# Strassen's seven products in the output projection of a hybrid attention and recurrence layer

## The chip, the core and the metric

The kernel runs on one NeuronCore of a Trainium2 chip. Its engines work side by side, each through its own queue in order: TensorE (PE, with its weight loads shown apart as PEld), VectorE (DVE), ScalarE (ACT), GpSimd (POOL) and SyncE (SP), which issues most of the transfers. The metric is the device time of one execution in microseconds (us), lower is better.

## The reference

One encoder layer, x of 512 positions by 2048 channels in float32. Cut to what matters here:

```python
h = rms_norm(x, norm_w)
q, k, v, g_attn, xr, g_lru = split(h @ w_in)          # w_in: 2048 x 4608
attn = attention_group(q, k, v)                        # 8 heads of 128, 2 key/value heads
lru = lru_group(xr)                                    # conv, gates, scans in both directions
mixed = concat([rms_norm(attn, attn_norm_w) * silu(g_attn),
                rms_norm(lru, lru_norm_w) * silu(g_lru)])   # 512 x 2048
out = x + mixed @ w_out                                # w_out: 2048 x 2048
```

## The kernel before

**Numbers.** Every product is float32 in three passes (`mm3`, L111): each operand is split into a high part (ScalarE rounds it, L168) and a low part (VectorE subtracts, L169), and TensorE adds high by high, high by low and low by high in one PSUM bank. PSUM is cut into four banks named pj, for the projections, and four named mm, for all else.

**Order.** The order of TensorE's instructions is that of the program text (a manual schedule, L599). The other engines are put in order by a scheduler when the program is built. Weights come in chunks of 256 rows by 512 columns (`wload`, L172), three raw buffers deep, and a loop over chunks (`proj_feat`, L239; `tok_block`, L259) gives way after each six matmuls of 512 columns. Such a group of six is called a step of filling here: `weave` (L274) runs a chain of other work and fills it with those steps.

**Stages.** (1) The rows of x are turned and normalised, and the first half of the recurrence's input is projected. (2) The recurrence runs between the projections of its second half, of keys and values, and of the queries. After the second block of queries `norm_rope` (L438) normalises and rotates it: per tile of 128 positions ScalarE squares (L446), GpSimd takes the root (`rsqrt_mean`, L218), and VectorE runs L451, L453 twice, L459 and L460. (3) `group_rstd` (L585) sums the recurrence's squares over channels on TensorE (L589), VectorE copies the result (L593) and GpSimd takes the root: r_l, one number for each position. (4) `attention` (L544) goes over 32 pairs of head and block of queries: scores (L507), a maximum (L509), exponentials (L512), a reciprocal (L513), a product on GpSimd (L514), transposes two pairs later (L521), products with the values one pair after that, as matmuls of 256 columns (L531). Between two pairs stand `STEPS = 3` steps of filling from the four blocks of gate projections (`all_gates`, L667). (5) r_a is made in the same way from the attention's squares (L688), the 16 blocks of the mixed features are split (`mixed`, L580), and the output projection runs (L694 to L708): for each of four blocks of 512 columns and each of the two groups, 96 matmuls of 512 columns go into four banks, and VectorE then adds them to x with r_l or r_a as the factor of each position:

```python
for c in range(DM // SEQ):
    for half, r in ((1, r_l), (0, r_a)):
        drain(tok_block(acc, w_out, half * 8 * P, c * SEQ, mh[half * 8 :], ml[half * 8 :], 8))
        ...
        nc.vector.scalar_tensor_tensor(part[t], acc[t], r[:, t : t + 1], part[t], ...)
```

The norm of each group is thus applied behind the product, and TensorE waits for neither r_l nor r_a.

## Time and profile before

| | us |
|---|---|
| median of 3 runs | 683.5 (683.4 to 683.67) |
| the profiled execution, its own time | 681.98 |
| its span, first to last instruction | 680.2 |
| TensorE busy within the span | 668.9 |
| VectorE, ScalarE, GpSimd busy | 407.5, 317.8, 74.4 |
| output projection, first to last matmul | 501.57 to 675.75 |

Durations of single instructions come from the profiled execution. A matmul's duration in it includes its way through the array, so that neighbours overlap: the distance from start to start is what a stream of them costs. A VectorE instruction, too, begins a little before the one ahead of it has ended.

### The profile page before, as it was taken

The page shows a single profiled execution, that of the slowest core. Times are in us where ns is not written, and L with a number is a line of the kernel's source. Part 1 is how long each engine was busy: PE and PEld are TensorE (multiplying, and loading weights), DVE is VectorE, ACT ScalarE, POOL GpSimd, SP SyncE. Part 2 cuts the span into 40 slices and gives each one's busy share as a digit, 9 for nine tenths or more (in the row PEclk, how much of TensorE's full clock was granted, in tenths as well). Part 3 has the DMA queues.
Part 4 walks back from the last instruction along what each step waited for, and adds up shares of the span by engine and source line. Part 5 has one row for each costly group of instructions (what it writes and reads, how often), then busy time and mean ns, then how long its engine had stood idle before and what let it go on. Part 6 is the DMA issues. An engine that isn't in the chain of part 4 may idle for free.

```text
span 680.2 us, 8576 instructions
## 1 busy us (share of the span) xinstructions
PE 668.9 (98%) x3154; PEld 555.2 (82%) x3154; DVE 407.5 (60%) x713; ACT 317.8 (47%) x593; POOL 74.4 (11%) x84
## 2 busy tenths in 40 slices
PE   8999999999989999999999999999999999999997
PEld 6888888887778888888888888888888888888885
DVE  5878697978495824856744774576475334443342
ACT  4534898588945427444634643464452222222220
POOL 0000001200150203201211111112000000000000
PEclk9999999999999999999999999999999999999999
DMA  8852242213123332222112122122256362522411
GB/s 281 279 155 75 82 131 89 66 62 94 62 75 112 100 98 81 93 64 65 61 63 92 51 74 63 62 63 76 81 173 202 109 227 93 155 93 93 160 58 63
DMA packets 43626, 71.01 MB, mean 104 GB/s; under 512 B 2760, under 2 KB 12864, under 8 KB 43584
## 3 DMA queue, kind: packets, MB, share of 16 engines
q1 hardware_dynamic: 43552, 70.45, 32.1%
q8 instruction: 25, 0.41, 0.3%
q14 instruction: 17, 0.14, 0.1%
q10 hardware_dynamic: 32, 0.01, 0.0%
HBM read 66.25 MB, written 4.19 MB: 104 GB/s over the span
## 4 chain that ended last, share of the span: by engine, by line
PE 85%; DVE 7%; ACT 4%; issue 2%; DMA 1%; SPq 0%; ACTq 0%; DVEq 0%
PE pj L113 24%; PE pj L112 24%; PE pj L114 24%; PE mm L114 3%; PE mm L113 3%; PE mm L112 3%; PE mm L521 2%; DVE b L399 2%; DVE wl L169 2%; DVE k L355 1%; PE mm L194 1%; ACT wh L168 1%; ACT b L388 1%; DMA b<-in_x_dram 1%; DVE b L396 1%
## 5 line engine op out<-in xcount | busy, mean ns | idle before, releaser
L169 DVE TENSOR_TENSOR wl<-wr,wh 128x512 fp32r<-128x512 f32 x208 | 145.4, 712 | 163.2 <-ACT wh L168 163.0
L168 ACT CAST wh<-wr 128x512 fp32r<-128x512 f32 x208 | 126.5, 620 | 209.5 <-PE pj L114 154.6
L112 PE MATMUL pj<-wh,x 128*128 128x512 f32 x448 | 175.1, 391 | 2.8 <-ACT ev L434 2.8
L113 PE MATMUL pj<-wl,x 128*128 128x512 f32 x448 | 174.8, 390 | 1.9 <-DVE wl L169 1.8
L114 PE MATMUL pj<-wh,x 128*128 128x512 f32 x448 | 174.5, 390 | 0.0
L112 PE MATMUL pj<-x,wh 128*128 128x512 f32 x384 | 152.9, 398 | 0.0
L114 PE MATMUL pj<-x,wl 128*128 128x512 f32 x384 | 150.0, 391 | 0.0
L113 PE MATMUL pj<-x,wh 128*128 128x512 f32 x384 | 149.9, 390 | 0.0
L112 PEld LDWEIGHTS pj<-wh,x 128*128 128x128 f32 x448 | 84.1, 188 | 21.3 <-ACT ev L434 3.6
L113 PEld LDWEIGHTS pj<-wl,x 128*128 128x128 f32 x448 | 84.1, 188 | 20.0 <-DVE wl L169 2.9
L114 PEld LDWEIGHTS pj<-wh,x 128*128 128x128 f32 x448 | 84.1, 188 | 17.4
L114 PEld LDWEIGHTS pj<-x,wl 128*128 128x128 f32 x384 | 72.1, 188 | 15.5
L113 PEld LDWEIGHTS pj<-x,wh 128*128 128x128 f32 x384 | 72.3, 188 | 13.9 <-issue 0.2
L112 PEld LDWEIGHTS pj<-x,wh 128*128 128x128 f32 x384 | 72.2, 188 | 14.0 <-issue 0.2
L523 ACT CAST b<-mm 128x512 fp32r<-128x512 f32 x32 | 18.8, 587 | 71.8 <-PE mm L521 71.8
L514 POOL TENSOR_SCALAR k<-k,sm 128x512 f32<-128x512 f32 x32 | 26.1, 817 | 157.4 <-DVE sm L513 139.1
L509 DVE TENSOR_REDUCE mx<-mm 128x1 f32<-128x512 f32 x32 | 22.0, 688 | 30.7 <-PE mm L114 30.6
L524 DVE TENSOR_TENSOR b<-mm,b 128x512 fp32r<-128x512 f32 x32 | 22.0, 689 | 10.5 <-ACT b L523 10.5
L408 POOL TENSOR_TENSOR hsum<-hsum,b 128x512 f32<-128x512 f32 x7 | 13.4, 1909 | 122.3 <-ACT b L407 122.3
L512 ACT ACTIVATE k<-mm,mx 128x512 f32<-128x512 f32 x32 | 22.1, 692 | 4.3 <-DVE mx L509 3.9
L372 ACT ACTIVATE b<-mm,vec 128x512 f32<-128x512 f32 x32 | 21.2, 687 | 1.2 <-PE mm L114 0.9
L320 DVE TENSOR_TENSOR ev<-pj,rbc 128x512 f32<-128x512 f32 x24 | 16.4, 689 | 6.5 <-PE pj L114 6.3
(136 smaller groups left out, 698.3 us busy)
## 6 DMA issues: line engine op xcount, KB each, us to landing
wr<-in_w_in_dram SPq DMA_DIRECT2D x71, 512.0 KB, 3.4
wr<-in_w_out_dram SPq DMA_DIRECT2D x32, 512.0 KB, 3.6
k<-in_x_dram SPq DMA_DIRECT2D x16, 256.0 KB, 5.2
out_dram<-k SPq DMA_DIRECT2D x16, 256.0 KB, 3.6
b<-in_x_dram SPq DMA_DIRECT2D x7, 512.0 KB, 8.3
k<-in_lru_wa_dram SPq DMA_DIRECT2D x8, 128.0 KB, 3.4
k<-in_lru_wx_dram SPq DMA_DIRECT2D x8, 128.0 KB, 2.9
b<-in_x_dram SPq DMA_DIRECT2D x2, 256.0 KB, 5.1
```

What stands on the lines that cost most here:

```text
L112: nc.tensor.matmul(acc, lh, rh, start=start, stop=False)
L113: nc.tensor.matmul(acc, lh, rl, start=False, stop=False)
L114: nc.tensor.matmul(acc, ll, rh, start=False, stop=stop)
L168: nc.scalar.copy(hi, raw[:, k, :])
L169: nc.vector.tensor_sub(lo, raw[:, k, :], f(hi))
L320: nc.vector.tensor_mul(e, a, rbc)
L372: nc.scalar.activation(dst[:, d, :], pg, AF.Sigmoid, bias=v1(bias + d * NB + n))
L509: nc.vector.tensor_reduce(mx, sc, axis=AX.X, op=ALU.max, negate=True)
L512: nc.scalar.activation(p, sc, AF.Exp, bias=mx, accum_out=sm)
L514: nc.gpsimd.tensor_scalar(p, p, sm, 0.0, op0=ALU.mult, op1=ALU.add)
L523: nc.scalar.copy(pth[:, :, tt], p3)
L524: nc.vector.tensor_sub(ptl[:, :, tt], p3, f(pth[:, :, tt]))
```

## The change

**Output projection** (`outputs`). The 16 blocks of 128 mixed features are taken in eight pairs. For one block of 512 output columns, a pair's product is that of a matrix of 2 by 2 blocks (position half by feature block) with one of 2 by 2 blocks (feature block by column half). Six of the eight pairs use seven products in place of eight, the other two use eight. Each product is made of 128-row stationary tiles and moving tiles of 256 columns. All products go into eight PSUM banks, four pj and four mm; the seven-product pairs share seven of them, and are combined after the sixth pair (L740 to L747). The operands need sums and differences of blocks: for the features (`build`) once, for the weights (`seven`, with `combine`) again for each chunk, on VectorE.

**Norms.** Since both groups now add into the same banks, r_l and r_a are multiplied into the features ahead of the product. `rows` (new) spreads r over all partitions: VectorE writes r times the identity (L260, four times), TensorE multiplies it by a matrix of ones (L262), VectorE copies the result to gbc (L263), and `normed` multiplies the pairs by it.

**Attention** has `STEPS = 2`; the fourth block of gates runs after it. **SBUF** is cut into pools that are opened and closed along the program, where a new tile waits only for the old tiles that it covers.

```diff
-STEPS = 3
+STEPS = 2
+    def rows(dst, col, dg):
+        for t in range(NT):
+            nc.vector.tensor_scalar(dg[:, t, :], ident, col[:, t : t + 1], None, op0=ALU.mult)
+        pb = mm()
+        nc.tensor.matmul(pb, ones, dg.rearrange("p t q -> p (t q)"), start=True, stop=True)
+        nc.vector.tensor_copy(dst, pb)
...
+    def normed(pair):
+        nc.vector.tensor_mul(pair, pair, gbc[:, None, :].broadcast_to([P, 2, SEQ]))
+    P1, Q6, Q5, Q7, P2, Q3, Q4 = (0, 0), (5, 5), (4, 3), (3, 4), (2, 2), (6, 1), (1, 6)
+    def combine(src, op):
+        res = pools["fin"].tile([P, 4, H], F32, tag="t4", bufs=2, name=nm("t4"))
+        a = nc.vector.tensor_tensor
+        if op == ALU.add:
+            a(res[:, 0:2], src[:, 1:3], src[:, 0:1].broadcast_to([P, 2, H]), op=op)
+            a(res[:, 2], res[:, 0], src[:, 2], op=op)
+            a(res[:, 3], res[:, 2], src[:, 3], op=op)
...
+    def seven(src, op, hi, lo):
+        src = halves(src)
+        res = combine(src, op)
+        for to, part in ((slice(0, 3), src[:, 1:4]), (slice(3, 7), res)):
+            nc.scalar.copy(hi[:, to], part)
+            nc.vector.tensor_sub(lo[:, to], part, f(hi[:, to]))
+    def outputs(work):
+        for c in range(DM // SEQ):
+            xt = pools["out"].tile([P, 4, 2, H], F32, tag="xt", bufs=1, name=nm("xt"))
...
+            for q, (ts_, cs) in enumerate(spots):
+                nc.sync.dma_start(xt[:, q], xf[ts_, cs].rearrange("(s p) e -> p s e", p=P))
+            acc = {k: pj() for k in (P1, Q6, Q5, Q7)} | {k: mm() for k in (P2, Q3, Q4, 0)}
...
+            for i, (r0, A) in enumerate(mixed):
...
+                if i < 6:
+                    for k in (P1, Q6, Q5, Q7, P2, Q3, Q4):
+                        for s in range(2):
+                            mult(k, s, ah, al, k[0], bh, bl, k[1], i == 5 and k in (P1, Q6, Q5, Q7))
+                else:
+                    for k, a, b_ in (
+                        (P2, (1, 3), (1, 3)), (Q3, (1, 3), (0, 2)),
+                        (Q4, (0, 2), (1, 3)), (0, (0, 2), (0, 2)),
+                    ):
...
+                if i == 5:
+                        nc.scalar.copy(comb[:, 0], acc[P1])
+                        nc.vector.tensor_sub(v2, acc[Q6], comb[:, 0])
+                        nc.vector.tensor_add(comb[:, 1], acc[Q5], v2)
+                        nc.vector.tensor_add(comb[:, 2], acc[Q7], comb[:, 1])
...
+                        nc.vector.tensor_add(xt, xt, comb)
+                for k, q in ((P2, 0), (Q3, 1), (Q4, 3), (0, 2)):
+                    nc.vector.tensor_add(xt[:, q], acc[k], xt[:, q])
+                    nc.sync.dma_start(of[ts_, cs].rearrange("(s p) e -> p s e", p=P), xt[:, q])
...
-    r_l = group_rstd(hsum, "r_l", NB * P)
-    fill = all_gates()
+    r = group_rstd(sums["l"], "r_l", NB * P)
+    rows(gbc, r, pools["rot"].tile([P, NT, P], F32, tag="sq", bufs=2, name=nm("sq")))
+    closed("rot", "rope")
+    opened("att", "right")
+    for pair in hp:
+        normed(pair)
+    fill = gates()
     weave(fill, attention(rots))
-    drain(fill)
-    r_a = group_rstd(asum, "r_a", NH * HD)
+    for _ in range(6):
+        next(fill)
+    r = group_rstd(sums["a"], "r_a", NH * HD)
+    next(fill)
+    rows(gbc, r, fin_s((P, NT, P)))
```

In the built program three places look as follows. The first is TensorE at the end of the second block of queries (its last matmul is the first row), before:

```order
L114 MATMUL pj_2082<-wh_2343,x_87_478 128x512
L589 MATMUL mm_2447<-ones,hsum 128x1 x4
L471 MATMUL mm_2457<-ident,ev_2003 128x128
L471 MATMUL mm_2457<-ident,ev_2005 128x128
L471 MATMUL mm_2457<-ident,ev_2007 128x128
```

and now:

```order
L145 MATMUL pj_2099<-wh_2360,x_87_489 128x512
L621 MATMUL mm_2464<-ones,hsum 128x1 x4
L262 MATMUL mm_2478<-sq_2473,ones 128x512
L507 MATMUL mm_2492<-ident,ev_2020 128x128
L507 MATMUL mm_2492<-ident,ev_2022 128x128
```

The matmul L262, which reads the tile sq_2473 that VectorE writes, has come between the sums of squares and the transposes of the queries.

The second place is VectorE at the same time, where ev_... are the four tiles of the second block of queries in `norm_rope`. Before, from the third and fourth tile's work on:

```order
L169 TENSOR_TENSOR wl_2570<-wr_2563,wh_2569 128x512
L460 TENSOR_TENSOR ev_2373<-ev_2373,sq_2429 128x512
L453 TENSOR_TENSOR sq_2435<-ev_2375,rq 128x8x32 x2
L451 TENSOR_TENSOR ev_2377<-ev_2377,rr_2412 128x512
L459 TENSOR_TENSOR ev_2375<-ev_2375,rq 128x512
L453 TENSOR_TENSOR sq_2441<-ev_2377,rq 128x8x32
L460 TENSOR_TENSOR ev_2375<-ev_2375,sq_2435 128x512
...
L459 TENSOR_TENSOR ev_2377<-ev_2377,rq 128x512
L169 TENSOR_TENSOR wl_2611<-wr_2608,wh_2610 128x512
...
L460 TENSOR_TENSOR ev_2377<-ev_2377,sq_2441 128x512
```

and now:

```order
L489 TENSOR_TENSOR sq_2452<-ev_2392,rq 128x8x32 x2
L487 TENSOR_TENSOR ev_2394<-ev_2394,rr_2429 128x512
L495 TENSOR_TENSOR ev_2392<-ev_2392,rq 128x512
L489 TENSOR_TENSOR sq_2458<-ev_2394,rq 128x8x32
L496 TENSOR_TENSOR ev_2392<-ev_2392,sq_2452 128x512
...
L260 TENSOR_SCALAR sq_2473<-ident,r_l 128x128
L495 TENSOR_TENSOR ev_2394<-ev_2394,rq 128x512
...
L496 TENSOR_TENSOR ev_2394<-ev_2394,sq_2458 128x512
L260 TENSOR_SCALAR sq_2473<-ident,r_l 128x128 x2
L263 COPY gbc<-mm_2478 128x512
L632 TENSOR_TENSOR hs_861<-hs_861,gbc 128x1024
```

The four instructions L260 that L262 reads stand at the end of the queries' normalisation (they write to the buffer of an earlier sq tile); the splits of the next weights (L169, now L200) have moved behind them.

The third place is TensorE where the output projection begins, before (x_923 and x_924 are the high and low part of a block of features):

```order
L113 MATMUL pj_4166<-x_87_477,wh_4530 128x512
L114 MATMUL pj_4166<-x_86_477,wl_4531 128x512
L589 MATMUL mm_4582<-ones,asum 128x1 x4
L112 MATMUL pj_4655<-wh_4661,x_923_4591 128x512
L113 MATMUL pj_4655<-wl_4662,x_923_4591 128x512
L114 MATMUL pj_4655<-wh_4661,x_924_4592 128x512
```

and now (mh and ml are those parts):

```order
L144 MATMUL pj_4364<-x_87_489,wh_4637 128x512
L145 MATMUL pj_4364<-x_86_488,wl_4638 128x512
L704 MATMUL pj_4683<-wh_4693,mh_4237 128x256
L704 MATMUL pj_4683<-wl_4694,mh_4237 128x256
L704 MATMUL pj_4683<-wh_4693,ml_4238 128x256
```

The matmuls have half the columns, and there are 1392 of them (464 of each of the three kinds) where there were 768.

More of the change, by code (lines that the diff above doesn't have):

```diff
@@ L640, in hybrid_kernel @@
     s1.close()
+    sums["l"] = pools["rope"].tile([P, SEQ], F32, tag="hsum", name="hsum")
     lru_consts()
@@ new lines, in hybrid_kernel, with build @@
+    fill = gates()
+    weave(fill, attention(rots))
+    for _ in range(6):
+        next(fill)
+    r = group_rstd(sums["a"], "r_a", NH * HD)
+    closed("att", "qkv")
+    opened("fin", "right")
+    next(fill)
+    rows(gbc, r, fin_s((P, NT, P)))
+    mixed = [[(NH + 2 * q) * P, None] for q in range(4)] + [[2 * q * P, None] for q in range(4)]
+    def build(i, pair, where, n=7):
+        mixed[i][1] = hi, lo = where(n)
+        if n == 7:
+            seven(pair, ALU.subtract, hi, lo)
+        else:
+            four(pair, hi, lo)
@@ new lines, in hybrid_kernel, with later @@
+    for q in range(4):
+        for _ in range(2):
+            next(fill, None)
+        build(q, hp[q], lambda n: kept(pools["fin"]))
+    drain(fill)
+    def later():
+        for pair in ap_[:2]:
+            normed(pair)
+        yield 6
+        todo = gate(late, ap_[:2], R_AN, fin_s)
+        for _ in range(3):
+            yield next(todo)
+        build(4, ap_[0], lambda n: [hring.tile([P, n, H], F32R, name=nm(t)) for t in ("mh", "ml")])
+        yield from todo
+        for pair in ap_[2:]:
+            normed(pair)
@@ new lines, in hybrid_kernel, with last_gates @@
+    acc = []
+    fill = proj_feat(C_GA + SEQ, acc)
+    weave(fill, later())
+    drain(fill)
+    gs = evac_bc(acc)
+    closed("xw")
+    opened("out", "left")
+    def last_gates():
+        yield
+        build(5, ap_[1], lambda n: kept(pools["out"]))
+        yield
+        todo = gate(gs, ap_[2:], R_AN + 4, fin_s)
+        for _ in range(3):
+            next(todo)
+        yield
+        build(6, ap_[2], lambda n: kept(pools["out"], n), 4)
+        drain(todo)
+        yield
+        build(7, ap_[3], lambda n: kept(pools["out"], n), 4)
+        yield
```

241 lines of the change are left out of this document (155 added, 86 removed).

## The prediction

> **What bounds the kernel now.** I read the page first: the busy times and the chain that ended last.
>
> ```profile
> span 680.2 us, 8576 instructions
> PE 668.9 (98%) x3154; PEld 555.2 (82%) x3154; DVE 407.5 (60%) x713; ACT 317.8 (47%) x593; POOL 74.4 (11%) x84
> PE 85%; DVE 7%; ACT 4%; issue 2%; DMA 1%; SPq 0%; ACTq 0%; DVEq 0%
> ```
>
> TensorE is busy for 668.9 of 680.2 us and makes up 85% of the chain. So a change pays only by taking work from TensorE, and anything that makes TensorE wait costs its full length. The second view is the output projection by itself: the stretch from its first to its last matmul, with the instructions that touch pj alone (columns: length, then busy time and count of PE, PEld, DVE).
>
> ```profile
> 501.57:675.75 174.18, 174.18 (x768) 144.07 (x768) 23.83 (x32) 0.00 (x0) 1.00 0.39 129
> ```
>
> 768 matmuls of 512 columns fill 174.18 us without a gap, 0.2268 us each, at full clock. The third view is the timeline of TensorE where the old kernel already runs the new shape, 256 columns with a stationary tile loaded for each (attention's values).
>
> ```profile
> 309.04 0.36 PE L112 MATMUL mm<-b,v 128*128 128x256 f32 x1
> 309.24 0.28 PE L113 MATMUL mm<-b,v 128*128 128x256 f32 x1
> 309.35 0.28 PE L114 MATMUL mm<-b,v 128*128 128x256 f32 x1
> ...
> 310.37 0.28 PE L114 MATMUL mm<-b,v 128*128 128x256 f32 x1
> 310.48 0.40 PE L112 MATMUL pj<-x,wh 128*128 128x512 f32 x1
> ```
>
> From the second matmul's start to that of the next group are 11 steps in 1.24 us: 0.113 us each. With its entry the group of 12 takes 1.44 us, 0.120 each.
>
> **1. The output projection.** Six pairs of seven products are 42 matmuls each, two pairs of eight are 48 each: 348 for a column block, 1392 in all. At half of 0.2268 us they take 157.9 us; the saving is 174.2 - 157.9 = **16.3 us**. Bounds: 17.3 us at 0.1127, 7.1 us at 0.120. I take the half, since a long stream is nearer to the inside of that group than to its entry.
>
> **2. Cover of that stream.** One column block is 39.5 us of TensorE, a seven-product pair 4.77 us. VectorE's work beside it comes from these groups.
>
> ```profile
> L169 DVE TENSOR_TENSOR wl<-wr,wh 128x512 fp32r<-128x512 f32 x208 | 145.4, 712 | 163.2 <-ACT wh L168 163.0
> L168 ACT CAST wh<-wr 128x512 fp32r<-128x512 f32 x208 | 126.5, 620 | 209.5 <-PE pj L114 154.6
> L396 DVE TENSOR_TENSOR b<-b,b 128x1024 f32<-128x1024 f32 x8 | 9.6, 1215 | 0.0
> L459 DVE TENSOR_TENSOR ev<-ev,rk 128x256 f32<-128x256 f32 x4 | 1.7, 416 | 0.0
> L704 DVE SCALAR_TENSOR_TENSOR k<-pj,r_a,k 128x512 f32<-128x512 f32 x16 | 12.0, 750 | 11.0 <-PE pj L114 10.9
> ```
>
> A chunk of weights for seven products takes 0.71 + 2 x 0.42 (sums) + about 0.96 (768 columns) + 1.22 = 3.7 us; six make 22.4, the other two 2.4. Combining takes 4 x 0.75, the sum of 2048 columns 2.4, the last four sums 3.0. Together 33 of 39.5 us: hidden, at 84% of VectorE, if weights run one pair ahead (the buffers hold three). ScalarE's casts, 1792 columns a chunk, are at most 2.2 us of 4.77. The banks pj are emptied during the two last pairs (10.9 us), the banks mm while the next block's four pj products run (2.7 us). SP's queue holds the writes of a finished block and the reads of x for the next ahead of the weights of its last pairs; those are needed some 30 us later. I allow **2 us** of waits in all (nothing to 12, if each of four column blocks loses 3). The features' sums are made beside the last gates; VectorE was busy for 22 of 40 us there:
>
> ```profile
> 460.00:500.00 40.00, 40.00 (x195) 33.62 (x194) 21.99 (x38) 18.00 (x32) 4.75 (x2) 1.00 0.29 94
> ```
>
> **3. The wait for r_l.** This is the expensive part. Before, TensorE went straight on after the sums of squares:
>
> ```profile
> 262.38 0.95 PE L589 MATMUL mm<-ones,hsum 128*128 128x1 f32 x8
> 263.19 1.07 PE L471 MATMUL mm<-ident,ev 128*128 128x128 f32 x8
> ```
>
> Now L262 stands between these two rows, and waits for VectorE's L260, which is queued behind nearly all of the normalisation of the second block of queries. That VectorE did in the same stretch of before:
>
> ```profile
> 262.82 0.69 DVE L451 TENSOR_TENSOR ev<-ev,rr 128x512 f32<-128x512 f32 x1 [4.33 <-ACT wh L168]
> ...
> 270.17 0.68 DVE L476 TENSOR_TENSOR b<-mm,b 128x512 fp32r<-128x512 f32 x1
> ...
> 272.64 1.29 DVE L169 TENSOR_TENSOR wl<-wr,wh 128x512 fp32r<-128x512 f32 x2
> ...
> 278.32 1.29 DVE L169 TENSOR_TENSOR wl<-wr,wh 128x512 fp32r<-128x512 f32 x2
> 279.53 0.69 DVE L460 TENSOR_TENSOR ev<-ev,sq 128x512 f32<-128x512 f32 x1
> ```
>
> ```profile
> 272.26 1.33 POOL L221 TENSOR_TENSOR rr<-rr,nhalf 128x4 f32<-128x4 f32 x1
> ```
>
> It ended at 280.2 us. Two L476 (1.2 us) and four L169 (2.4) are now behind L260, and four L260 (0.9) come in: 277.5. From the other side: GpSimd's last root ended at 273.6 and now comes up to 2 us earlier; behind it VectorE has four instructions of 0.6, two of 0.34 and four L260, 4 us: 275.6 to 277.6. TensorE is free at 263.2, so it idles about **13.5 us**, nothing else being queued ahead of L262. Bounds: 11.7 (VectorE from 262.8 on without any wait: four tiles of 2.5, two splits of 0.6, four L260) and 17.9 (280.2 + 0.9). Behind the wait stand the queries' transposes, eight steps of filling and all of attention; VectorE itself loses nothing, and its five instructions behind L262 (6 us) end within those steps (10.9 us).
>
> Each L262 costs more than one slot. The same product for the first norm, before:
>
> ```profile
> 53.66 1.02 PE L234 MATMUL mm<-k,ones 128*128 128x512 f32 x2
> 54.12 0.80 PE L112 MATMUL pj<-x,wh 128*128 128x512 f32 x1
> 54.76 0.39 PE L113 MATMUL pj<-x,wh 128*128 128x512 f32 x1
> ```
>
> From its start to that of the third row are 1.10 us, with one matmul of 0.23 in them: 0.87 us. Two of them: **1.7 us**.
>
> **4. A cold clock.** The windows around the kernel's end (last column but two: granted clock) and two rows from its start:
>
> ```profile
> 676.00:678.00 2.00, 0.00 (x0) 0.00 (x0) 0.70 (x1) 0.00 (x0) 0.00 (x0) 1.00 0.56 219
> 678.00:680.20 2.20, 0.00 (x0) 0.00 (x0) 0.00 (x0) 0.00 (x0) 0.00 (x0) 0.53 0.10 39
> ```
>
> ```profile
> 1.12 2.95 PE L606 MATMUL mm<-ones 128*128 128x256 bf16 x13 [1.12 <-POOL ones L120]
> 7.42 0.49 PE L606 MATMUL mm<-ones 128*128 128x256 bf16 x3
> ```
>
> The clock falls to about half some 2 us after the last matmul. Cold, 13 matmuls take 2.95 us, about 0.21 from start to start; the three later ones, with 0.28 for the way through, about 0.1. So after 13 us of idleness TensorE runs at half rate for 3 to 4 us and loses half of it: **1.8 us** (1.5 to 2). The Trainium skill's page "TensorE: Matmul & The Clock Gate" (Part 1) says that an idle window of about 3.4 us halves the clock and 3.4 us of work restore it, which speaks against this change as well; by it the loss would be 1.7 us, and the sum 0.1 lower. The trace, a fall after some 2 us and about 3 us cold, agrees but for the first.
>
> **5. The wait for r_a.** The second pair of sums and L262 has one step of filling (1.36 us) between. The chain:
>
> ```profile
> 509.22 0.16 DVE L593 COPY r_a<-mm 128x4 f32<-128x4 f32 x1
> ```
>
> ```profile
> 509.47 0.56 POOL L220 TENSOR_SCALAR r_a<-r_a 128x4 f32<-128x4 f32 x1 [30.47 <-DVE r_a L593]
> 510.12 1.34 POOL L221 TENSOR_TENSOR r_a<-r_a,nhalf 128x4 f32<-128x4 f32 x1
> ```
>
> Copy to root is 2.24 us, four L260 0.9, handing over 0.2: 3.3 - 1.36 = **2.0 us**, 1.2 if GpSimd takes as long as it did for r_l, 2.7 if a split of weights is in VectorE's way.
>
> **6. At nothing.** Attention with two steps between pairs does the same work. Softmax still has two pairs' time before its transposes, 5.4 us of filling alone, for three instructions of 0.7 to 0.8 us on three engines:
>
> ```profile
> L509 DVE TENSOR_REDUCE mx<-mm 128x1 f32<-128x512 f32 x32 | 22.0, 688 | 30.7 <-PE mm L114 30.6
> L512 ACT ACTIVATE k<-mm,mx 128x512 f32<-128x512 f32 x32 | 22.1, 692 | 4.3 <-DVE mx L509 3.9
> L514 POOL TENSOR_SCALAR k<-k,sm 128x512 f32<-128x512 f32 x32 | 26.1, 817 | 157.4 <-DVE sm L513 139.1
> ```
>
> If that cover went, 32 pairs would wait. The pools' waits fall on tiles last read a block earlier. The waits that TensorE has now stay, at 2.8 and 1.8 us:
>
> ```profile
> PE pj L112 <- ACT ev L434: 2.8, 2, 1.7
> PE pj L113 <- DVE wl L169: 1.8, 1, 1.8
> ```
>
> VectorE's and ScalarE's order there differs slightly; I give it 2 us either way. The end is as before: one sum and a write behind the last matmul.
>
> **The sum.** -16.3 + 13.5 + 1.7 + 1.8 + 2.0 + 2.0 = +4.7 us: a span of 684.9. The profiled execution took 681.98, 1.8 over its span; so 686.7. The median of the runs, 683.5, stands 1.5 above the profiled one: **688.2 us**. No change means within 0.2% (682.1 to 684.9), about what a measurement of this kernel can tell. Its own range: -17.3 + 11.7 + 1.7 + 1.5 + 1.2 + 0 = -1.2 at the best, and with 0.120 us for a matmul and 17.9 us of wait about +19; by ends that don't fall together, 684 to 695.
>
> **Rivals.**
>
> *Faster: r_l comes in time.* If TensorE's wait at L262 were only r_l's own chain, copy, root and L260, as for r_a, it would be 3 us, with no cold clock: -16.3 + 3 + 1.7 + 2 + 2 = -7.6, **676 us**. It decides from a wait of about 7.5 us on: below that the kernel is faster by over 0.2%. For it: L260 needs nothing of the queries. Against it: VectorE takes its instructions in the built order, where L260 comes last. A tenth or so.
>
> *Slower by far: the stream of 256 columns doesn't hold its pace.* The trace shows it for 12 matmuls in a row, now 1392 follow each other. At 0.120 us, the group with its entry, the projection takes 167.0 us: +9.1, **697 us**. Against it: each weight load of that group starts with the matmul ahead of it, and nothing in it slows from the second to the twelfth. The Trainium skill's page "TensorE: Matmul & The Clock Gate" ("Wait — 56ns, not 53.3ns?") has the sequencer spend about 62 ns on each MATMUL when instructions aren't decoded in hardware; if a weight load cost as much (my estimate), a pair would take 124 ns, and the time be 703 us.
>
> *Slower: VectorE bounds the projection.* Its 84% leave 6.5 us for each block; if waits for ScalarE, banks or transfers in its one queue take more than that, TensorE waits. At 3 us lost for each block, 12 in place of 2: **698 us**.
>
> That the change doesn't do what it says is excluded: the built program has the 1392 matmuls.
>
> **Chances.** The forecast 0.62, r_l in time 0.13, the slow stream 0.12, VectorE 0.11, the rest 0.02. Of the forecast's 0.62, 0.51 lie above 684.9, 0.09 within and 0.02 below; the first rival gives 0.12 to faster and the two others all to slower: 0.15 faster, 0.11 the same, 0.74 slower. The range, 680 to 699, leaves out the first rival's lower part and the worst of the others.
>
> **What would show it.** Right: one idle stretch of TensorE of 12 to 15 us at 263 us that VectorE's L260 ends, a clock near half behind it, a second wait of 2 us, and an output projection of 158 to 162 us. Wrong: no such stretch; or matmuls of 256 columns further apart than 0.115 us; or waits for wl at each column block.

## The result and the profile after

The changed kernel takes 692.3 us (median of 4 runs, 691.4 to 693.1) against 683.5 for the kernel before beside it (682.2 to 683.7): a ratio of 1.0133, interval 1.0115 to 1.0151. It is slower, as forecast, by 9 us; the forecast of 688.2 was 4 us too low. Executions of the kernel before are of two kinds, 681.4 to 682.7 us at a mean granted clock of 0.998 to 1.000 and 683.0 to 683.9 us at 0.996 or 0.997, and its median lies among the second, its profiled execution among the first. The profiled execution took 692.67, its span is 690.6, 10.4 more than before's.

The page of the changed kernel: the span, the busy times, and TensorE over 40 slices of the span with its granted clock below it, both in tenths.

```profile
span 690.6 us, 9880 instructions
PE 664.9 (96%) x3782; PEld 579.2 (84%) x3782; DVE 482.8 (70%) x815; ACT 336.0 (49%) x585; POOL 71.9 (10%) x84
...
PE   8999999998999992999999999999999999999997
...
PEclk9999999999999996899999999999999999999999
```

TensorE's busy time fell by only 4.0 us, and one slice is nearly empty. The view of waits, longest first (in total, times, longest), says who left it empty; the second wait was there before, as L112 for ScalarE's L434, the third is the one for r_a:

```profile
PE mm L262 <- DVE sq L260: 14.2, 1, 14.2
PE pj L143 <- ACT kv L470: 2.7, 2, 1.6
PE mm L262 <- DVE s L260: 1.4, 1, 1.4
```

The timeline of TensorE at that place (start, length, at the end the idle time and who ended it), to be laid beside the two rows of before in step 3 of the prediction:

```profile
262.15 0.95 PE L621 MATMUL mm<-ones,hsum 128*128 128x1 f32 x8
277.34 2.08 PE L262 MATMUL mm<-sq,ones 128*128 128x512 f32 x2 [14.24 <-DVE sq L260]
279.21 1.92 PE L507 MATMUL mm<-ident,ev 128*128 128x128 f32 x8
280.77 0.78 PE L143 MATMUL pj<-x,wh 128*128 128x512 f32 x1
...
282.17 0.40 PE L143 MATMUL pj<-x,wh 128*128 128x512 f32 x1
```

TensorE idles 14.24 us before L262. What follows is slow until 282.17: the same eight transposes took 0.82 us in the late run below and take 1.56 here, the three matmuls 1.40 where 0.78 is usual. GpSimd's timeline has r_l ready at 269.1, and VectorE's shows it spread only among the last instructions of the normalisation:

```profile
268.07 1.06 POOL L252 TENSOR_TENSOR r_l<-r_l,nhalf 128x4 f32<-128x4 f32 x1
```

```profile
275.21 0.28 DVE L260 TENSOR_SCALAR sq<-ident,r_l 128x128 f32<-128x128 f32 x1
...
276.20 0.69 DVE L496 TENSOR_TENSOR ev<-ev,sq 128x512 f32<-128x512 f32 x1
276.81 0.48 DVE L260 TENSOR_SCALAR sq<-ident,r_l 128x128 f32<-128x128 f32 x2
```

Its windows: first the output projection, then the stretches around the wait (length, busy times of PE, PEld, DVE, ACT and POOL, granted clock, DMA share, GB/s):

```profile
521.38:686.67 165.29, 165.29 (x1393) 165.24 (x1391) 124.59 (x167) 55.86 (x64) 0.00 (x0) 1.00 0.44 138
...
264.00:266.00 2.00, 0.00 (x0) 0.00 (x0) 2.00 (x5) 1.81 (x9) 1.00 (x2) 0.76 0.00 0
...
280.00:282.00 2.00, 2.00 (x9) 1.81 (x8) 1.97 (x3) 1.17 (x2) 0.00 (x0) 0.50 0.00 0
282.00:284.00 2.00, 2.00 (x10) 1.61 (x9) 2.00 (x3) 0.00 (x0) 0.00 (x0) 0.97 0.00 0
```

The clock is at half from 265 to 282. The projection has no gap, at full clock, and takes 165.3 us: 8.9 less than the 174.2 of before, not 16.3 less. A matmul of 256 columns takes 0.1187 us in the mean, and in long stretches of the timeline exactly 0.12:

```profile
560.13 0.28 PE L704 MATMUL mm<-wh,ml 128*128 128x256 f32 x1
560.25 0.28 PE L704 MATMUL mm<-wh,mh 128*128 128x256 f32 x1
560.37 0.28 PE L704 MATMUL mm<-wl,mh 128*128 128x256 f32 x1
```

By stages, between the same instructions of both timelines:

| stage | before | after | difference |
|---|---|---|---|
| start to the sums for r_l (L589, now L621) | 262.38 | 262.15 | -0.2 |
| from there to the queries' first transposes | 0.81 | 17.06 | +16.2 |
| from there to the first matmul of the projection | 238.38 | 242.17 | +3.8 |
| projection | 174.18 | 165.29 | -8.9 |
| behind it | 4.45 | 3.93 | -0.5 |
| span | 680.2 | 690.6 | +10.4 |

Two causes are thus to be tested: the idle stretch, and a stream of narrow matmuls that gives back nearly half of its saving.

### The profile page after: what moved, and what is told of

It reads as the page before. It is cut to its first block, busy times and chain, and to the rows that moved or that the text cites. A ratio compares the mean times of both kernels' runs of the same rounds, so it can differ in the third digit from the quotient of the medians.

```text
span 690.6 us, 9880 instructions
## 1 busy us (share of the span) xinstructions
PE 664.9 (96%) x3782; PEld 579.2 (84%) x3782; DVE 482.8 (70%) x815; ACT 336.0 (49%) x585; POOL 71.9 (10%) x84
## 4 chain that ended last, share of the span: by engine, by line
PE 88%; DVE 5%; ACT 3%; issue 1%; POOL 1%; DMA 1%; SPq 0%; POOLq 0%; ACTq 0%
PE pj L144 17%; PE pj L145 17%; PE pj L143 17%; PE mm L704 14%; PE pj L704 10%; PE mm L145 3%; PE mm L143 3%; PE mm L144 3%; PE mm L554 2%; DVE b L434 1%; DMA b<-in_x_dram 1%; PE mm L225 1%; PE mm L507 1%; ACT wh L199 1%; DVE wl L200 1%
## 5 line engine op out<-in xcount | busy, mean ns | idle before, releaser
L200 DVE TENSOR_TENSOR wl<-wr,wh 128x512 fp32r<-128x512 f32 x144 | 98.0, 700 | 67.6 <-ACT wh L199 61.6
L143 PE MATMUL pj<-wh,x 128*128 128x512 f32 x192 | 75.2, 392 | 2.7 <-ACT kv L470 2.7
L704 PE MATMUL mm<-wh,ml 128*128 128x256 f32 x272 | 76.6, 282 | 0.0
L704 PE MATMUL mm<-wh,mh 128*128 128x256 f32 x272 | 76.6, 282 | 0.0
L704 PE MATMUL mm<-wl,mh 128*128 128x256 f32 x272 | 76.5, 281 | 0.0
L144 PE MATMUL pj<-wl,x 128*128 128x512 f32 x192 | 75.0, 390 | 1.1 <-DVE wl L200 1.1
L145 PE MATMUL pj<-wh,x 128*128 128x512 f32 x192 | 74.9, 390 | 0.0
L704 PE MATMUL pj<-wh,ml 128*128 128x256 f32 x192 | 54.1, 282 | 0.0
L704 PE MATMUL pj<-wh,mh 128*128 128x256 f32 x192 | 54.0, 281 | 0.0
L704 PE MATMUL pj<-wl,mh 128*128 128x256 f32 x192 | 53.8, 280 | 0.0
L704 PEld LDWEIGHTS mm<-wl,mh 128*128 128x128 f32 x272 | 51.7, 190 | 0.0
L143 PEld LDWEIGHTS pj<-wh,x 128*128 128x128 f32 x192 | 36.0, 188 | 11.0 <-ACT kv L470 3.6
```

Source lines behind the costliest of these rows:

```text
L143: nc.tensor.matmul(acc, lh, rh, start=start, stop=False)
L144: nc.tensor.matmul(acc, lh, rl, start=False, stop=False)
L145: nc.tensor.matmul(acc, ll, rh, start=False, stop=stop)
L200: nc.vector.tensor_sub(lo, raw[:, k, :], f(hi))
L704: nc.tensor.matmul(acc[k][:, s, :], lh[:, a, ts_], rh[:, b_, :], start=k in fresh, stop=last and s == 1 and j == 2, skip_group_check=True,)
```

## The experiments

In these kernels the lines of the changed one are shifted by one where a constant was added (L262 is L263 there).

### The idle stretch

**Late spreading of r_l.** The spreading and the scaling by it move 20 steps of filling down TensorE's order.

```diff
-    rows(gbc, r, pools["rot"].tile([P, NT, P], F32, tag="sq", bufs=2, name=nm("sq")))
+    r_l = r
...
-    for pair in hp:
-        normed(pair)
...
-            for _ in proj_feat(c0, acc):
+            for m, _ in enumerate(proj_feat(c0, acc)):
+                if n == 0 and m == LATE:
+                    rows(gbc, r_l, k2(shape=(P, NT, P)))
+                    for pair in hp:
+                        normed(pair)
```

Expected: 

> The changed kernel, but the spreading of r_l (L260, L262) and the scaling of the LRU's outputs come 20 steps of filling later on TensorE; the sums of squares stay where they are. If the idle stretch costs what its stage lost (14.2 us of wait, 1.4 of cold clock, 1.0 of the cold L262): 692.3 - 16.6 = 675.7 us. Theory of a new wait: VectorE's last instruction of the normalisation of the queries still ends at about 276.5 us, and two splits of weights and two of queries are queued behind it, while TensorE would reach the first scores at 275.5: some 3 us of the wait come back there, 678.7 us. Rival (the wait only moves as a whole, TensorE being held by VectorE's queue anyway): 688 or more.

Measured: 684.3 us (10 runs, 683.6 to 685.2), ratio to before 1.0022, interval 1.0012 to 1.0033; 8.1 less than the changed kernel. The stretch is gone, and half of it has come back at other places. Its timeline of TensorE, at the first scores and 37 us later:

```profile
274.69 0.39 PE L146 MATMUL pj<-x,wl 128*128 128x512 f32 x1
277.73 0.50 PE L144 MATMUL mm<-kt,b 128*128 128x512 f32 x1 [2.65 <-ACT b L512]
...
279.65 0.79 PE L146 MATMUL mm<-kt,b 128*128 128x512 f32 x1 [1.18 <-DVE b L513]
...
318.79 0.63 PE L555 MATMUL mm<-ident,k 128*128 128x128 f32 x4 [1.56 <-DVE b L558]
```

From 274.69 to 282.67 TensorE does what takes 2.3 us in the kernel before, 5.7 us more. Of these, 4.3 pass until the third matmul of the first scores has started: that is the new wait of the expectation, longer than its 3 us. The other 1.4 were not expected. Behind this wait the clock was at half again, from 279.10 to 282.51, as the windows show (columns as above):

```profile
278.00:280.00 2.00, 0.82 (x3) 0.38 (x3) 2.00 (x4) 0.17 (x1) 0.00 (x0) 0.77 0.00 0
280.00:282.00 2.00, 2.00 (x8) 1.62 (x8) 0.93 (x3) 0.65 (x2) 0.00 (x0) 0.50 0.94 252
```

Two more losses were not foreseen: 0.6 us where L263 now stands, beyond its own warm cost, and 1.8 us behind the four scalings in a row on VectorE (L633, 4.63 us from 311.61 on), the last row of the timeline. Of the 16.6 us that go, 8.1 come back; the span fell by 8.5.

**The same with its cover moved too.** 11 steps instead of 8 before the first scores, 4 instead of 6 before the sums for r_a, 3 instead of 1 between these and their spreading.

```diff
-        yield 8
+        yield 11
...
-    for _ in range(6):
+    for _ in range(4):
         next(fill)
     r = group_rstd(sums["a"], "r_a", NH * HD)
...
-    next(fill)
+    for _ in range(3):
+        next(fill)
```

Expected: 

> As the run before, and the two ends of attention shifted: 11 steps of filling instead of 8 before the first scores, 4 instead of 6 before the sums of r_a and 3 instead of 1 between these and the spreading of r_a. If waits are what these steps cover: the 3 us at the first scores and the 1.43 us before the second L262 go, about 674 us; 675 if the cover at the end is now short by as much. Rival (those waits are not covered by more filling): the same as the run before.

Measured: 679.8 us, ratio to before 0.9957, interval 0.9945 to 0.9970: faster than before. The waits at the first scores and at both L263 are gone, so those steps do cover them. Of the 5.8 us left against the 674, some 3.7 are waits in attention, mostly behind VectorE again (1.56 us at 307.80, 0.85 at 337.56, 1.3 at 413); the rest is not assigned.

**Two steps in attention, alone in the kernel before.**

```diff
-STEPS = 3
+STEPS = 2
```

Expected: 

> The kernel before with one number changed: two steps of filling instead of three between pairs of attention; the steps left over follow behind attention. The prediction gave this nothing, up to 2 us either way: 683, between 681 and 685. Rival (softmax's chain is no longer covered, and each of 32 pairs waits some tenths): 687 or more.

Measured: 682.7 us against 682.1 (the means are 682.7 and 682.6), ratio 1.0002, interval 0.9993 to 1.0012. No change. Its profiled execution shows how little idleness halves the clock: a wait of 1.83 us, which the kernel before has too (1.8 us, in the view of waits in step 6 of the prediction), is followed here by half clock from 201.84 to 205.25, and by none in the profiled execution of before. First the row that ends the wait, then a window behind it:

```profile
200.66 0.49 PE L113 MATMUL pj<-wl,x 128*128 128x512 f32 x1 [1.83 <-DVE wl L169]
```

```profile
202.00:205.00 3.00, 3.00 (x9) 2.32 (x8) 3.00 (x12) 0.00 (x0) 0.00 (x0) 0.50 0.62 175
```

### The pace of narrow matmuls

The theories of the pace are named by letters, A to C in the first expectation, D to F further down; E is one idea in the second measurement and another in the third and fourth. The pace is the mean distance from one matmul's start to the next.

**Place and length.** The stream alone, other engines idle; in place of the kernel's body stands, for each segment:

```python
for r in range(96):
    o = (r // 3 % half) * n
    nc.tensor.matmul(acc[:, o : o + n], st[:, sm * P : (sm + 1) * P], yt[:, ym * n : (ym + 1) * n], ...)
```

Expected: 

> This kernel computes nothing of the reference: it loads one block of x, copies it (as fp32r) to two moving tiles, ylo at the bottom and yhi at the top of SBUF, and to seven stationary tiles, sa to sg, at 25, 49, 85, 93, 109, 149 and 189 KB, and then runs segments of 96 matmuls, each with a weight load of its own, all other engines idle: 256 columns for each of the 14 pairs of places, then 128, 192, 320, 384, 448 and 512 columns with the stationary tile far (sf) and near (sa), then 256 columns with the same moving tile each time, the same stationary tile, both, and one region of a bank. It measures the disputed pace by itself. Theory A (place): the distance depends on where the two operands lie; about 0.120 us from start to start when they lie in the same part of SBUF, 0.116 to 0.118 when they lie apart, and streams of 128 and 192 columns are faster than that. Theory B (issue): every matmul with its load takes 0.117 to 0.120 us of the sequencer, whatever the place, and 128 and 192 columns take as long as 256. Theory C (other engines' traffic slows TensorE in the projection): here, with idle engines, all 256-column segments go at 0.1134.

Its timeline of TensorE (96 matmuls to a row; the distance from one start to the next, by 96, is the pace):

```profile
104.11 11.68 PE L121 MATMUL ylosg<-ylo,sg 128*128 128x256 f32 x96
115.63 11.68 PE L121 MATMUL yhisa<-yhi,sa 128*128 128x256 f32 x96
...
196.27 10.84 PE L121 MATMUL wafar<-ylo,sf 128*128 128x128 f32 x96
206.94 10.88 PE L121 MATMUL wanear<-ylo,sa 128*128 128x128 f32 x96
```

All 14 places go at 0.1200, so theory A falls as stated, and theory C too: with nothing else running the stream isn't at 0.1134. 128 and 192 columns take 0.111 to 0.112 (theory B's floor, lower than it said), 320 take 0.147, 384 0.173, 512 0.227. From 256 columns up a matmul thus costs about 0.42 ns for each column and some 0.013 us besides ((0.227 - 0.120) / 256; 0.120 - 256 x 0.00042), whatever its width (448 stand out with 0.207, 0.006 more).

**Eight products for all pairs, 256 columns.** With `NSEV = 0` every pair takes the branch of eight products: features and weights are split in four pieces each (`four`), without Strassen's sums, and a column block goes into four banks (an extract).

```diff
+NSEV = 0
...
-            acc = {k: pj() for k in (P1, Q6, Q5, Q7)} | {k: mm() for k in (P2, Q3, Q4, 0)}
+            acc = {k: (mm, pj)[c % 2]() for k in (P2, Q3, Q4, 0)}
...
-                    if i < 6:
+                    if i < NSEV:
                         bh, bl = wkept(7)
                         seven(raw, ALU.add, bh, bl)
...
-                if i < 6:
+                if i < NSEV:
...
-        mixed[i][1] = hi, lo = where(n)
-        if n == 7:
+        mixed[i][1] = hi, lo = where(4)
+        if NSEV:
             seven(pair, ALU.subtract, hi, lo)
```

Expected: 

> The changed kernel with eight products for all pairs of row blocks, still in pieces of 256 columns: no sums of halves on VectorE, 1536 matmuls in the projection instead of 1392, VectorE's work there cut to less than half. If the pace of 0.1187 us belongs to the stream of narrow matmuls (theories A and B): the projection takes 1536 x 0.1187 = 182.3 us, 17.0 more than the changed kernel, 709 us. If VectorE's and ScalarE's load in the projection slows the stream (theory C), the pace goes back to 0.1134: 174.2 us, 8.9 more, 701 us.

Measured: 708.5 us, as expected if the pace belongs to the stream of narrow matmuls. The window of its projection:

```profile
520.02:702.40 182.38, 182.38 (x1536) 182.34 (x1535) 1.00 0.40 125
```

0.1187 us a matmul once more, with VectorE at less than half of its work there. So Strassen saves 17.1 us of projection against this, and cutting the matmuls in half had cost 8.2 (182.4 against 174.2).

**Eight products, 512 columns, in the changed kernel's pools.**

```diff
-                            for j in range(2):
-                                mult(k, s, ah, al, a[j], bh, bl, b_[j], i == 7 and j == 1)
+                        for k in range(2):
+                            rh, rl = (
+                                w[:, 2 * k : 2 * k + 2, :].rearrange("p j e -> p (j e)")
+                                for w in (bh, bl)
+                            )
+                            mm3(acc[a, s], ah[:, 2 * k + a, ts_], al[:, 2 * k + a, ts_], rh, rl, ...)
```

Expected: 

> The changed kernel with eight products for all pairs of row blocks and 512 columns for a matmul, so 768 matmuls as in the kernel before, with the changed kernel's pools, order and waits. If the projection's time is only the number of matmuls times their pace, 768 x 0.2268 = 174.2 us, 8.9 more than the changed kernel: 701 us, and 7.4 below the eight products at 256 columns (708.5). If the new pools or buffers cost TensorE something in the projection that the narrow stream hides, more than 701.

Measured: 704.5 us. The window of its projection, all engines:

```profile
520.89:698.11 177.22, 177.22 (x769) 144.03 (x767) 56.41 (x72) 36.05 (x36) 0.00 (x0) 1.00 0.41 127
```

There is no gap; each matmul takes 0.2308 us instead of 0.2268, 3.0 us more in all. The trace says where: of the 32 groups of 24 matmuls, one for each pair of a weight and a feature buffer, 15 go at 0.2267 to 0.2286 and 17 at 0.2330 to 0.2335. The same 15 pairs take 0.1195 or more at 256 columns in the changed kernel, and the other 17 take 0.1184 or less there. So the pace goes with the pair of buffers, in both shapes, and the faster pairs of the one are the slower ones of the other. The next measurement says what it is about a pair.

**Alignment.** As in the measurement of place and length, but with one place for each operand and a start that moves by `so` or `yo` bytes (the remainder of an operand is here what is left of its start address divided by 256 bytes):

```diff
-            ym = 0 if fix_y else (r * 5) % per
-            sm = 0 if fix_s else (r * 3) % 16
+            ym, sm = yo // 4 + r * 5 % per * n, so // 4 + r * 3 % 16 * P
```

Expected: 

> Like the first measurement of the pace (nothing of the reference is computed, other engines idle), but now the place is fixed and the start of the stationary tiles is moved against that of the moving tiles, which are multiples of 1 KB apart, by 0 to 448 bytes in 18 segments of 96 matmuls of 256 columns; then the moving tiles by 16 to 128 bytes; both by 64; then 512 columns at seven offsets and 128, 192, 320, 384 and 448 columns at 0 and 64. In the first measurement all tiles began at the same remainder by 128 bytes, and 256 columns took 0.1200 us everywhere. In the changed kernel's projection the remainders of weights and features are equal where it goes at 0.120 and 32 bytes apart where it goes at 0.1165 to 0.118; in the attention of the kernel before they are 64 apart and it goes at 0.1134. Theory D (relative alignment by 128 bytes sets the pace): 0.120 at 0, 128, 256, 384; about 0.117 at 32, 96, 160, 224; 0.1133 at 64, 192, 320, 448; at 64 also 512 columns fall, to 0.220. Theory E (the faster matmuls of the kernels come from something else, such as what other engines do): 0.1200 in all segments of 256 columns.

Its timeline of TensorE: stationary tiles shifted by 0 and by 64 bytes, then 512 columns at 0 and 64. The longer a row, the slower its 96 matmuls.

```profile
23.46 11.67 PE L106 MATMUL segaa<-y,s 128*128 128x256 f32 x96
...
91.46 11.05 PE L106 MATMUL segag<-y,s 128*128 128x256 f32 x96
...
295.17 21.95 PE L106 MATMUL segay<-y,s 128*128 128x512 f32 x96
...
361.12 22.56 PE L106 MATMUL segbb<-y,s 128*128 128x512 f32 x96
```

Alignment does set the pace, so theory E falls. But theory D has the period wrong: 0.1133 comes at 64 and 320 bytes, while 192 and 448 give 0.118 and most others 0.116 to 0.119; 0, 112, 160 and 256 give 0.120. Each of the four offsets that was tried again 256 bytes further gave the same pace. And 512 columns don't gain: 0.227 at 0, 16 and 256 bytes, 0.232 to 0.234 at 32 to 128. These are the two paces of the eight wide products, whose 0.2308 is thus a mixture of good and bad pairs; moving the operands of that kernel was not tried by itself.

**In the kernel: weights and features 64 bytes apart, and at the same remainder.** Each pair of tiles gets 256 spare bytes, and its start is shifted (shown for weights).

```diff
-        return [
-            pool.tile([P, 7, H], F32R, tag=f"{t}{i}", bufs=1, name=nm(t))[:, :n]
-            for t in ("wh", "wl")
-        ]
+        t = pool.tile([P, 14 * H + 64], F32R, tag=f"w{i}", bufs=1, name=nm("w"))
+        hi, lo = pair_of(t, 7, WAT, "left" if i else "right")
+        return hi[:, :n], lo[:, :n]
```

Expected, 64 apart: 

> The changed kernel, but with the projection's operands shifted within their tiles so that all weights begin at 128 by 256 bytes and all features at 192; nothing else moves, and the long wait stays. In the second measurement of the pace 256 columns took 0.1133 us at that pair of remainders and 0.118 to 0.120 at nearly all others. If it is these remainders that set the pace in the kernel: 1392 x 0.1133 = 157.7 us for the projection instead of 165.3, so 692.3 - 7.6 = 684.7 us. Rival (in the kernel other engines' accesses spoil it): 0.117 to 0.119 as now, and 691 to 693 us.

Expected, the same: 

> As the run before, with weights and features both at 128 by 256 bytes, where the measurement showed 0.1200 us. If the remainders set the pace: 167.0 us for the projection, 1.8 more than the changed kernel, 694 us. Rival: as the changed kernel, 692.3.

Measured: 691.4 us and 694.2. The windows of the projection, first of the one and then of the other:

```profile
522.05:686.15 164.10, 164.10 (x1392) 163.90 (x1391) 1.00 0.45 139
```

```profile
521.61:688.81 167.20, 167.19 (x1392) 166.99 (x1391) 1.00 0.44 136
```

At the same remainder the pace is 0.120, as expected. At 64 bytes it is a uniform 0.1178 (164.0 / 1392): the projection gains 1.2 us, not 7.6, and pace and time are those that the rival named. Whether the rival's cause, other engines' accesses, is the right one, the next two measurements ask.

**The kernels' own order and addresses, idle engines.** One tile fills SBUF, and operands are taken from it by address:

```python
ah, al = (at(x + a * 1024 + s * 512, P) for x in (fh, fl))
bh, bl = (at(x + b * 1024, H) for x in (wh, wl))
three = [(ah, bh, o), (ah, bl, o), (al, bh, o)]
```

Expected: 

> A third measurement of the pace with idle engines (nothing of the reference is computed), now with the order of operands, the indices and the addresses of the kernels' own projection: three matmuls (high x high, high x low, low x high) for each half and product, 84 to a segment. First come seven pairs of addresses of the changed kernel, four of the aligned kernel, then 16 offsets between weights and features, the same with the second and third matmul exchanged, and 64 combinations in which the high and low parts are shifted separately. Theory D (addresses alone set the pace): the pairs that go at 0.1198 to 0.120 in the changed kernel (weights and features on one side of SBUF) do so here, those at 0.116 to 0.118 likewise, and the aligned kernel's addresses give its 0.1178 instead of the 0.1133 of the second measurement, because here a stationary tile is loaded twice in a row and high and low parts alternate. Theory E (the other engines' accesses keep the kernel from 0.1133): the aligned kernel's addresses give 0.1133 here.

Its timeline of TensorE (84 matmuls to a row): three of the changed kernel's pairs of addresses, then two of the aligned kernel's.

```profile
65.25 10.06 PE L115 MATMUL segac<-o 128*128 128x256 f32 x84
75.14 10.24 PE L115 MATMUL segad<-o 128*128 128x256 f32 x84
85.22 10.06 PE L115 MATMUL segae<-o 128*128 128x256 f32 x84
...
115.12 9.69 PE L115 MATMUL segah<-o 128*128 128x256 f32 x84
124.65 9.68 PE L115 MATMUL segai<-o 128*128 128x256 f32 x84
```

For the changed kernel's addresses theory D holds: the second to the seventh pair go at 0.118, 0.118, 0.120, 0.118, 0.118 and 0.120, where the kernel has 0.117, 0.117, 0.120, 0.118, 0.118 and 0.120 for the same pairs (the first waited once for ScalarE, which was still filling SBUF, and then went at 0.120, as in the kernel). No other engine is needed for its pace. For the aligned kernel's addresses it fails: 0.1133 here. Of 16 offsets 64 bytes alone gave 0.1136, the rest 0.117 to 0.120. With the second and third matmul exchanged, 64 bytes gave 0.1178, so the offset alone does not make the fast pace. Of the 64 combinations three went at 0.1133 to 0.1143, all others at 0.116 to 0.121.

**Company.** The same at the aligned addresses, with one thing added to a segment:

```python
if "v" in ops:
    for _ in range(14):
        nc.vector.tensor_sub(vc, va, vb)
...
for _ in range(lead):
    nc.tensor.matmul(acc[0], at(F, P), at(W, SEQ), start=True, stop=True)
```

Expected: 

> A fourth measurement of the pace (nothing of the reference is computed), at the addresses of the aligned kernel, which went at 0.1133 us with idle engines and one bank of PSUM but at 0.1178 in the kernel. Segments of 168 matmuls in the projection's order add one thing each: three matmuls of 512 columns ahead (leadwide), six banks in turn (sixbanks), VectorE busy with subtractions in SBUF (vector), ScalarE with copies (scalar), loads from memory (loads), weights and features changing their buffers after each pair of row blocks (turning), this with six banks, and all together; plain segments stand between. Theory E (other engines' accesses keep the kernel from 0.1133): plain segments 0.1133, vector, scalar or loads 0.116 to 0.120. Theory F (the sequence keeps it: banks, changing buffers, or how the stream is entered): vector, scalar and loads stay at 0.1133, and leadwide, sixbanks or turning go at 0.1178.

Its timeline of TensorE, and below it its windows for plainb, for vector, and for the segment in which all come together (length, busy times of PE, PEld, DVE, ACT and POOL, clock, DMA share, GB/s):

```profile
43.28 19.20 PE L146 MATMUL plaina<-o 128*128 128x256 f32 x168
62.33 0.85 PE L134 MATMUL leadwide<-o 128*128 128x512 f32 x3
63.02 19.95 PE L146 MATMUL leadwide<-o 128*128 128x256 f32 x168
...
102.59 19.95 PE L146 MATMUL plainb<-o 128*128 128x256 f32 x168
```

```profile
102.59:122.38 19.79, 19.79 (x171) 19.79 (x169) 4.29 (x7) 0.17 (x1) 0.00 (x0) 1.00 0.00 1
122.38:142.16 19.78, 19.78 (x170) 19.78 (x169) 17.92 (x16) 0.17 (x1) 0.00 (x0) 1.00 0.00 1
...
300.46:320.24 19.78, 19.78 (x170) 19.78 (x169) 17.92 (x16) 14.90 (x15) 0.00 (x0) 1.00 0.43 133
```

The first plain segment takes 19.05 us, 0.1133 a matmul. Then three matmuls of 512 columns pass, and from there on every segment takes 19.78 or 19.79, 0.1178: the plain ones again too, and those with VectorE, ScalarE or loads not a hundredth more. So the 0.1178 needs no other engine, and theory F holds in one of its forms: what ran just ahead can set the pace, and the stream stays in it. This was seen once, in one execution. The projection is entered from matmuls of 512 columns, which fits its 0.1178. Whether other engines, banks or changing buffers could bring a stream down from 0.1133 as well can't be told from this, since they were tried only after the pace had dropped.

### All together

The late spreading with its cover, the aligned operands, the values and keys of attention aligned likewise, and the four scalings spread over 24 steps (an extract, against the late spreading with its cover).

```diff
-LATE = 20
+VO, KO = 16, 32
+LATE, SCALE = 20, [(0, 24), (0, 28), (1, 8), (1, 16)]
...
+                if (n, m) in SCALE:
+                    normed(hp[SCALE.index((n, m))])
```

Expected: 

> The run with the late spreading of r_l and shifted ends of attention (679.8 us), with the projection's operands aligned as in the first run of this call, the values and keys of attention aligned likewise (values against probabilities 64 bytes apart, keys at the remainder of the queries), and the four scalings of the LRU's outputs by r_l spread over 24 steps instead of one place. If these add up: 679.8 - 7.6 for the projection, 1 for the 192 matmuls of values at 0.1133 instead of 0.1185, 1 to 3 for waits of attention behind VectorE's four scalings in a row: 668.5 to 670.5 us. Rival (the gains don't add, a wait takes their place): 673 or more.

Measured: 676.8 us (676.4 to 676.9), ratio to before 0.9915, interval 0.9900 to 0.9929: faster than both kernels, but 6 to 8 us above the expectation. Its projection takes 164.1 us, as in the aligned kernel, since its 0.1178 is the same; all but one of the 16 groups of values stayed at 0.117 or above; only the waits in attention fell, by some 1.9 us.

## Why the prediction was right, and where it was wrong

The direction was right, the time lies in the range, and the waits came where and as they were forecast. By the prediction's own signs it is split: the idle stretch, its releaser and the cold clock are among what was to show it right, while 0.1187 us a matmul and a projection of 165.3 us are beyond the 0.115 and the 158 to 162 that it had set. Term by term, by the rows above:

| term | forecast | measured |
|---|---|---|
| the projection's matmuls (step 1) | -16.3 | -8.9 |
| waits within the projection (step 2) | +2.0 | 0 |
| wait for r_l (step 3) | +13.5 | +14.2 |
| two L262, warm (step 3) | +1.7 | +1.7 |
| cold clock (step 4) | +1.8 | +2.4 |
| wait for r_a (step 5) | +2.0 | +1.4 |
| all else (step 6) | 0 | -0.4 |
| sum | +4.7 | +10.4 |

**Steps 3 to 5, right.** One stretch of 14.2 us, ended by VectorE's L260, inside the 12 to 15 that were to show it. The built order alone told this: L260 stands behind the normalisation. The cold clock cost 1.0 in L262 (1.87 against 0.87), 0.7 in the transposes and 0.6 in three matmuls: it held for 4.8 us after work came back, not for the 3 to 4 of the forecast (and for 2.9 to 6.1 in four other kernels with the same wait, so 2.4 is one draw). The late run shows that the stretch is the cause, and that half of what it cost comes back elsewhere, most of it as a wait for VectorE, unless more steps cover it.

**Step 2, too careful.** VectorE is busy for 124.6 of 165.3 us there, 75% instead of 84, and TensorE waits for nothing.

**Step 1, the term that failed.** "I take the half, since a long stream is nearer to the inside of that group than to its entry." What failed is the size of the matmul term: it measured -8.9 us, near the low end of the stated bounds (7.1 to 17.3). The pace inside that group belonged to its operands' places and to what ran before it, not to matmuls of 256 columns as such. The long stream goes at 0.1187, and a stream of equal remainders at 0.120 with nothing beside it. The trace of before held the warning: of the 16 groups of values, six go at 0.118 from their second matmul on, among them the first:

```profile
297.32 0.28 PE L113 MATMUL mm<-b,v 128*128 128x256 f32 x1
297.44 0.28 PE L114 MATMUL mm<-b,v 128*128 128x256 f32 x1
...
298.50 0.28 PE L114 MATMUL mm<-b,v 128*128 128x256 f32 x1
```

These are ten steps in 1.18 us. I had quoted one group, a fast one. With 0.1187 for step 1 the sum would have been +12 and the median 695.6. That the forecast missed by 4 us and not by 7.4 is luck: 2.0 us of waits were not there, and this kernel's median lies 0.3 below its profiled execution, where 1.5 above had been carried over from before; the other terms give 0.5 the other way.

**The rivals.** That "the stream of 256 columns doesn't hold its pace" is what happened, nearly in full (167.0 us of projection forecast, 165.3 measured), and 0.12 was too low a chance for it; its time of 697 had the same 2 us of waits in it. The rule of the Trainium skill's page "TensorE: Matmul & The Clock Gate" ("Wait — 56ns, not 53.3ns?") that I set beside it, 124 ns for a pair by my estimate, is not borne out: 128 and 192 columns go at 0.111 to 0.112, so that no floor of 124 ns binds a stream of 256. "r_l comes in time" and "VectorE bounds the projection" didn't happen.

**What stays open.** Why the aligned kernel goes at 0.1178 when the same addresses can go at 0.1133: the entry from wide matmuls does it in the measurement, but a kernel that enters its projection in another way was not tried. The traces say that wide matmuls are not the whole answer. In the run of all together, 15 groups of values stand right behind transposes, all shifted to the same remainders, and 14 of them go at 0.118 and one at 0.113. And in the measurement of alignment 0.1133 came some 70 us after the last wide matmuls, with slower streams of 256 columns between. Nor is it known by what rule the remainders act.

## What to carry to other kernels

Half the columns are not half the time of a matmul: here each cost some 0.013 us besides its columns, so that nearly half of Strassen's saving went into 624 more matmuls. Before a short group is taken for a long stream, look at all its instances and at what lies ahead of them. And a norm that moves from behind a product to the front of the next stage needs its place in the order of every engine: here the same change with r_l spread 20 steps later, and its cover moved along, turns 1.3% slower into 0.4% faster.

## What the runs showed of the hardware

- A matmul of 256 columns with its own weight load takes 0.1133 to 0.120 us at full clock, by the remainders of both operands' addresses (64 bytes apart was best, equal remainders were among the worst), by the order of the three matmuls or by what ran just before; 512 columns take 0.227 at equal remainders and up to 0.234 at others. With 128 and 192 columns the pace stays at 0.111 to 0.112. The Trainium skill's page "TensorE: Matmul & The Clock Gate" ("Wait — 56ns, not 53.3ns?") gives a warm matmul its columns at 2.4 GHz and 2.5 ns more, 0.109 and 0.216 us by my estimate; the runs here are 0.004 to 0.018 above that.
- VectorE at 91%, ScalarE at 75% and loads of 133 GB/s at once changed the pace of that stream, at 0.1178, by less than 0.0001 us a matmul.
- In the changed kernel the granted clock fell to half some 1.9 us after the last matmul (265.04 by the mean of 0.76 from 264 to 266, the last having ended at 263.10) and was full again 4.8 us after the next began. These times are not fixed: in the four other kernels with the same wait of 14.2 us the fall came 2.8 to 3.9 us after the last matmul and the return 2.9 to 6.1 us after the next. The clock stayed at half for 17.07 us in three of these five and for 13.65 in two, and for 3.41 after the shorter waits in the late run and in the kernel of before with two steps: five, four and one times 3.41 us. A wait of 1.83 us was enough to bring that about once.
